# Batched 64x64 matrix products: transposing the second to fourth a tile on VectorE, instead of the third to sixth

## The chip, the cores and the metric

The kernel runs on one core of one Trainium2 chip. The metric is the device time in microseconds (us) of one execution; lower is better. TensorE, VectorE, ScalarE, GpSimd and SyncE are the core's engines; the profile calls them PE (PEld for its weight loads), DVE, ACT, POOL and SP.

## The reference

```python
a = randn(1024, 64, 64)   # float32
b = randn(1024, 64, 64)   # float32
out = np.matmul(a, b)     # 1024 products of 64x64 by 64x64, float32
```

Each input and the output hold 16.78 MB. The products are taken of bf16 casts, with float32 sums.

## The kernel before

**Tiling.** b and the output are cut into 16 steps t of 64 matrices, 1.05 MB each (`n_t = 16`). a is cut into 8 tiles s of 128 matrices (`n_s = 8`), 2.1 MB each, and tile s serves the steps 2s and 2s + 1. The text writes a(s), b(t) and store(t) for these. "The second to fourth a tile" are s = 1, 2, 3; "the third to sixth" are s = 2 to 5.

**Loads.** `load_a(s)` (L70) makes four DMAs: three quarters of the tile go from GpSimd's queue (q0 in the profile), cast to bf16 on the way, into a_sb (L74), and the fourth from SyncE's queue (q1) as float32 into a_raw (L78). Both pools have three buffers (`A_AHEAD = 3`). `load_first_a` (L81) loads tile 0 as float32 into two output buffers. `load_b(t)` (L94) loads one float32 tile b_sb, for even t from SyncE's queue, for odd t from ScalarE's (q10), into one of three buffers (`B_AHEAD = 3`). Every DMA stands in the program of the engine that issues it, so it goes only after that engine has passed the instructions ahead of it, and when its buffer is free.

**From a to the weights.** Each product needs a transposed. There are two ways to it:

- Over TensorE: `regroup(s)` (L100) puts the four quarters side by side into a_bf, with two VectorE copies (L109 from a_sb, L112 from a_raw with a cast; tile 0 has casts of its own, L106). Then `transpose(s, j)`, j = 0 and 1 (L133), makes 8 TensorE transposes (L138) of pairs of bf16 numbers taken as one float32, and two ScalarE copies (L141) from PSUM (at_ps) to at_sb.
- On VectorE: `transpose_dve(s, half)` (L116) transposes two of the four quarters with one VectorE instruction each (L128, 32x32 blocks). The fourth quarter (h = 3), loaded as float32, is first cast to bf16 by ScalarE (L126).

`ON_DVE` lists the tiles that take the second way. From at_sb, `spread(t)` (L146) copies with VectorE into at_bd, one of two block-diagonal buffers whose zeros are set once: 4 copies of 32 x 1024 (L164) for a tile that came over TensorE, 8 copies of 32 x 512 (L154) for one from VectorE.

**Cast, product, output.** `cast(t)` (L169) casts b_sb to b_bf on VectorE (step 0 on ScalarE, the last step in four pieces on both). `multiply(t)` (L187) makes 64 TensorE products in two halves into two PSUM buffers (o_ps), and copies each half to an output buffer o_sb with four copies (L206). These run on ScalarE; of the second half, two go to VectorE in odd steps past the VectorE tiles:

```python
if half and t % 2 and t > 2 * max(ON_DVE):
    copies[2:] = [nc.vector.tensor_copy] * 2
```

so in steps 11 and 13 before. Step 15, the last, has copies of its own on both engines, in quarters. `store(t)` (L183) writes o_sb from GpSimd's queue one step later (`HOLD = 2`); the last two outputs go in smaller pieces, from SyncE's and ScalarE's queues.

**Order.** `manual_schedule()` keeps the order of the program on each engine; nothing is reordered. In step t come, in this order: spread(t + 1), cast(t + 1), load_b(t + 3), in even steps load_a(t/2 + 4) (while there are tiles left) and the second half of tile t/2 + 1's TensorE transposes, multiply(t), then work on tile s + 2 (in even steps regroup or the first VectorE half, in odd steps the first TensorE transposes or the second VectorE half), and store(t - 1). Step 0 prepares tile 1 after its product, and step 1 all of tile 2 if VectorE takes it. GpSimd's queue thus holds load_a(4), store(0), load_a(5), store(1), store(2), load_a(6) and so on; SyncE's a_raw and the even b tiles in turn.

Of the kernel before, what the change touches and what calls it, by code (L numbers as in the profile page):

```python
# [13 lines left out]
def kernel(  # L14
# [21 lines left out]
    B_AHEAD = 3  # L36
    N_BD = 2
    HOLD = 2
    ON_DVE = (2, 3, 4, 5)

    a_v = a.rearrange("(s g h) (mp v) k -> s h g mp (v k)", h=4, g=32, v=16)
    b_v = b.rearrange("(t g h) (kp u) n -> t (h kp) g (u n)", h=4, g=16, u=2)
# [19 lines left out]
    a_tiles, b_tiles, abf_tiles, at_tiles, bbf_tiles = {}, {}, {}, {}, {}  # L62
# [7 lines left out]
    def load_a(s):  # L70

        a_sb = a_pool.tile([128, 3, 16, 64], bf16, name="a_sb")
        for h in range(3):
            nc.gpsimd.dma_start(  # L74
                out=a_sb[:, h, :, :].rearrange("p v k -> p (v k)"), in_=a_v[s, h], single_packet=True
            )
        a_raw = a_pool.tile([128, 16, 64], fp32, name="a_raw")
        nc.sync.dma_start(out=a_raw[:].rearrange("p v k -> p (v k)"), in_=a_v[s, 3])  # L78
        a_tiles[s] = a_sb, a_raw

    def load_first_a():  # L81

        raw = [
            o_pool.tile([128, 8, 2, 2, 64], fp32, name="o_sb")[:].rearrange(
                "p gh j wl n -> p (gh j wl n)"
            )
            for _ in range(2)
        ]
        parts = [raw[h % 2][:, 1024 * (h // 2) : 1024 * (h // 2) + 1024] for h in range(4)]
        for h in range(4):  # L90
            (nc.scalar if h % 2 else nc.sync).dma_start(out=parts[h], in_=a_v[0, h])
        a_tiles[0] = parts

    def load_b(t):  # L94
        b_sb = b_pool.tile([128, 16, 128], fp32, name="b_sb")
        queue = nc.scalar if t % 2 else nc.sync
        queue.dma_start(out=b_sb[:], in_=b_v[t])  # L97
        b_tiles[t] = b_sb

    def regroup(s):  # L100
        a_sb = a_tiles.pop(s)
        a_bf = work.tile([128, 16, 4, 64], bf16, name="a_bf")
        if s == 0:
            for h in range(4):
                copy = nc.scalar.copy if h % 2 else nc.vector.tensor_copy
                copy(a_bf[:, :, h, :], a_sb[h].rearrange("p (v k) -> p v k", v=16))  # L106
        else:
            cast_sb, raw = a_sb
            nc.vector.tensor_copy(  # L109
                a_bf[:, :, 0:3, :], cast_sb[:].rearrange("p h v k -> p v h k")  # L110
            )
            nc.vector.tensor_copy(a_bf[:, :, 3, :], raw[:])  # L112
        abf_tiles[s] = a_bf
        at_tiles[s] = work.tile([128, 32, 4, 4, 4], fp32, name="at_sb")

    def transpose_dve(s, half):  # L116
        cast_sb, raw = a_tiles[s]
        if half == 0:
            at_tiles[s] = work.tile([128, 4, 8, 4, 4, 4], fp32, name="at_sb")
        for h in (2 * half, 2 * half + 1):  # L120
            rows = cast_sb[:, h, :, :] if h < 3 else None
            if h == 3:
                rows = work.tile([128, 16, 4, 64], bf16, name="a_bf")[:, 0:4, :, :].rearrange(
                    "p x y k -> p (x y) k"
                )
                nc.scalar.copy(rows, raw[:])  # L126
            pairs = rows.rearrange("p v k -> p (v k)").bitcast(fp32)
            nc.vector.transpose(  # L128
                at_tiles[s][:, h].rearrange("p g w mp vo -> p w vo g mp"),
                pairs.rearrange("p (vo w kp) -> p w vo kp", vo=4, w=4),  # L130
            )

    def transpose(s, j):  # L133
        a_cols = abf_tiles[s][:].rearrange("p v h k -> p v (h k)").bitcast(fp32)
        for wl in range(2):
            at_ps = t_psum.tile([128, 4, 128], fp32, name="at_ps")
            for vo in range(4):
                nc.tensor.transpose(  # L138
                    at_ps[:, vo, :], a_cols[:, 4 * vo + 2 * j + wl, :], identity[:]
                )  # L140
            nc.scalar.copy(  # L141
                at_tiles[s][:, :, 2 * j + wl, :, :],
                at_ps[:].rearrange("p vo (g mp) -> p g mp vo", mp=4),
            )

    def spread(t):  # L146
        bd = bd_tiles[t % N_BD]
        at_sb = at_tiles[t // 2]
        for h in range(4):
            rows = slice(32 * h, 32 * h + 32)  # L150
            if t // 2 in ON_DVE:
                for i in range(2):
                    block = 32 * (2 * (t % 2) + i)
                    nc.vector.tensor_copy(  # L154
                        bd[rows, 8 * i : 8 * i + 8, :, h, :, :].rearrange(
                            "p g w mp vo -> p (g w) (mp vo)"
                        ),
                        at_sb[block : block + 32, h].rearrange(
                            "p g w mp vo -> p (g w) (mp vo)"
                        ),  # L160
                    )
            else:
                half = slice(16 * (t % 2), 16 * (t % 2) + 16)
                nc.vector.tensor_copy(  # L164
                    bd[rows, :, :, h, :, :].rearrange("p g w mp vo -> p (g w) (mp vo)"),
                    at_sb[rows, half].rearrange("p g w mp vo -> p (g w) (mp vo)"),
                )

    def cast(t):  # L169
        b_bf = work.tile([128, 16, 128], bf16, name="b_bf")  # L170
        b_sb = b_tiles.pop(t)
        if t < n_t - 1:
            (nc.vector.tensor_copy if t else nc.scalar.copy)(b_bf[:], b_sb[:])  # L173
        else:
            for gq in range(4):
                rows = slice(4 * gq, 4 * gq + 4)
                if gq % 2:
                    nc.vector.tensor_copy(b_bf[:, rows, :], b_sb[:, rows, :])
                else:
                    nc.scalar.copy(b_bf[:, rows, :], b_sb[:, rows, :])  # L180
        bbf_tiles[t] = b_bf

    def store(t):  # L183
        for piece in held.pop(t):
            piece()

    def multiply(t):  # L187
# [20 lines left out]
        for half in range(2):  # L208
# [19 lines left out]
            if not last:  # L228
                copies = [nc.scalar.copy] * 4
                if half and t % 2 and t > 2 * max(ON_DVE):  # L230
                    copies[2:] = [nc.vector.tensor_copy] * 2
# [7 lines left out]
    with tc.manual_schedule():  # L239
        load_first_a()  # L240

        nc.vector.memset(warm[:, 0:1], 0.0)
        nc.scalar.copy(warm[:, 1:2], warm[:, 0:1])
        load_b(0)
        load_b(1)
        nc.vector.memset(bd_tiles[0][:], 0.0)  # L246
        make_identity(nc, identity)
        nc.gpsimd.memset(bd_tiles[1][:, 0:8], 0.0)
        load_a(1)
        load_b(2)  # L250
        nc.gpsimd.memset(bd_tiles[1][:, 8:16], 0.0)
        load_a(2)
        regroup(0)
        transpose(0, 0)
        transpose(0, 1)
        spread(0)
        cast(0)
        for t in range(n_t):
            s, half = t // 2, t % 2
            if t + 1 < n_t:  # L260
                spread(t + 1)
                cast(t + 1)
            if t + B_AHEAD < n_t:
                load_b(t + B_AHEAD)
            if half == 0 and 0 < s < n_s - 1 - A_AHEAD:
                load_a(s + 1 + A_AHEAD)
            if half == 0 and 0 < s < n_s - 1 and s + 1 not in ON_DVE:
                transpose(s + 1, 1)
            multiply(t)
            if t == 0:  # L270
                regroup(1)
                load_a(A_AHEAD)
                load_a(A_AHEAD + 1)
                transpose(1, 0)
                transpose(1, 1)
            if t and s + 2 in ON_DVE and (half or s):
                for part in [0, 1] if t == 1 else [half]:
                    transpose_dve(s + 2, part)
                if half:
                    a_tiles.pop(s + 2)  # L280
            elif half == 0 and 0 < s and s + 2 < n_s:
                regroup(s + 2)
            elif half == 1 and s + 2 < n_s:
                transpose(s + 2, 0)
            if t >= HOLD - 1:
                store(t - HOLD + 1)
        for t in range(n_t - HOLD + 1, n_t):
            store(t)
# [30 lines left out]
```

## Time and profile before

| | before |
|---|---|
| time, median of 3 runs | 134.39 us (134.0 to 134.44) |
| profiled execution: its time / its span | 134.24 / 132.1 us |
| VectorE busy | 100.7 us (76%) |
| ScalarE busy | 89.2 us (68%) |
| TensorE busy, weight loads | 63.2 us (48%), 60.5 us (46%) |
| GpSimd busy | 32.0 us (24%) |
| DMA: q0 (GpSimd), q1 (SyncE), q10 (ScalarE) | 50.6%, 30.8%, 20.0% of 16 engines' span |
| read from and written to memory | 33.55 MB and 16.78 MB |
| TensorE clock granted, mean | 0.693 |

The profile's page gives busy times, the span in 40 slices (3.3 us each; digits are tenths of busy time), the DMA queues, the chain of waits that ended last, and groups of instructions ("out<-in", partitions x elements, count, busy time, mean ns of one, idle time of the engine before them and what ended it). L numbers are lines of the kernel. Each b tile takes 14.4 to 26.3 us from its issue to its landing; the first multiplication starts at 21.09 us.

### The profile page before, as it was taken

The page shows a single profiled execution, that of the slowest core. Times are in us where ns is not written, and L with a number is a line of the kernel's source. Part 1 is how long each engine was busy: PE and PEld are TensorE (multiplying, and loading weights), DVE is VectorE, ACT ScalarE, POOL GpSimd, SP SyncE. Part 2 cuts the span into 40 slices and gives each one's busy share as a digit, 9 for nine tenths or more (in the row PEclk, how much of TensorE's full clock was granted, in tenths as well). Part 3 has the DMA queues.
Part 4 walks back from the last instruction along what each step waited for, and adds up shares of the span by engine and source line. Part 5 has one row for each costly group of instructions (what it writes and reads, how often), then busy time and mean ns, then how long its engine had stood idle before and what let it go on. Part 6 is the DMA issues. An engine that isn't in the chain of part 4 may idle for free.

```text
span 132.1 us, 2719 instructions
## 1 busy us (share of the span) xinstructions
PE 63.2 (48%) x1088; PEld 60.5 (46%) x1088; DVE 100.7 (76%) x150; ACT 89.2 (68%) x159; POOL 32.0 (24%) x43
## 2 busy tenths in 40 slices
PE   0006406990733701909190737359709834677700
PEld 0006306980733701909190737259709734676700
DVE  5930399209999915999989998999999998598730
ACT  2225524999893790583989197929999996728970
POOL 8991000420074000702061302040203040312000
PEclk9999999999686555555555555555995995555555
DMA  3999999999999999999999999999999999999996
GB/s 83 351 336 310 309 313 277 288 301 327 326 305 385 371 308 298 395 385 396 327 282 357 402 395 347 296 326 387 399 392 394 394 392 387 398 399 396 364 324 201
DMA packets 19020, 44.99 MB, mean 341 GB/s; under 512 B 1088, under 2 KB 3136, under 8 KB 19008
## 3 DMA queue, kind: packets, MB, share of 16 engines
q0 software_dynamic: 6832, 20.19, 50.6%
q1 hardware_dynamic: 7120, 14.68, 30.8%
q10 hardware_dynamic: 5056, 9.96, 20.0%
q8 instruction: 8, 0.13, 0.4%
q14 instruction: 4, 0.03, 0.1%
HBM read 33.55 MB, written 16.78 MB: 381 GB/s over the span
## 4 chain that ended last, share of the span: by engine, by line
DMA 37%; DVE 27%; ACT 13%; PE 9%; issue 8%; ACTq 2%; SPq 1%
DMA b_sb<-in_b_dram 31%; DVE at_bd L154 11%; ACT o_sb L206 11%; DMA o_sb<-in_a_dram 6%; DVE b_bf L173 6%; PE o_ps L218 5%; DVE at_bd L164 4%; PE at_ps L138 3%; DVE at_sb L128 3%; DVE a_bf L109 1%; DVE a_bf L112 1%; ACTq L97 1%; ACT a_bf L126 1%; ACT a_bf L106 1%; ACT at_sb L141 1%
## 5 line engine op out<-in xcount | busy, mean ns | idle before, releaser
L206 ACT COPY o_sb<-o_ps 64x512 f32<-64x512 f32 x116 | 67.4, 581 | 19.2 <-PE o_ps L218 16.1
L218 PEld LDWEIGHTS <-at_bd 128*128 128x128 bf16 x1024 | 50.5, 125 | 52.9 <-DVE b_bf L173 44.7
L218 PE MATMUL o_ps<-b_bf,at_bd 128*128 128x64 bf16 x960 | 49.1, 231 | 49.4 <-DVE b_bf L173 42.7
L164 DVE COPY at_bd<-at_sb 32x1024 f32<-32x1024 f32 x32 | 23.2, 724 | 12.7 <-ACT at_sb L141 11.9
L154 DVE COPY at_bd<-at_sb 32x512 f32<-32x512 f32 x64 | 27.9, 436 | 1.3
L195 POOL DMA_DIRECT2D out_dram<-o_sb x14 | 15.5, 1108 | 47.5 <-ACT o_sb L206 30.7
L74 POOL DMA_DIRECT2D a_sb<-in_a_dram x21 | 12.4, 606 | 39.8 <-DVE at_sb L128 26.4
L173 DVE CAST b_bf<-b_sb 128x2048 bf16<-128x2048 f32 x14 | 17.2, 1227 | 6.4 <-DMA b_sb<-in_b_dram 6.0
L138 PE MATMUL at_ps<-identity,a_bf 128*128 128x128 f32 x64 | 11.2, 349 | 11.2 <-ACT a_bf L106 11.2
L138 PEld LDWEIGHTS at_ps<-identity,a_bf 128*128 128x128 f32 x64 | 10.3, 188 | 11.1 <-issue 11.1
L128 DVE STREAM_TRANSPOSE at_sb<-a_sb 128x512 f32<-128x512 f32 x12 | 12.0, 1062 | 0.0
L141 ACT COPY at_sb<-at_ps 128x512 f32<-128x512 f32 x16 | 8.5, 594 | 2.1 <-PE at_ps L138 2.0
L106 ACT CAST a_bf<-o_sb 128x1024 bf16<-128x1024 f32 x2 | 2.1, 1044 | 5.2 <-DMA o_sb<-in_a_dram 5.2
L128 DVE STREAM_TRANSPOSE at_sb<-a_bf 128x512 f32<-128x512 f32 x4 | 4.2, 1053 | 0.7 <-ACT a_bf L126 0.7
L126 ACT CAST a_bf<-a_raw 128x1024 bf16<-128x1024 f32 x4 | 4.2, 1046 | 0.7 <-DMA a_raw<-in_a_dram 0.6
L173 ACT CAST b_bf<-b_sb 128x2048 bf16<-128x2048 f32 x1 | 1.9, 1898 | 3.7 <-DMA b_sb<-in_b_dram 3.7
L206 DVE COPY o_sb<-at_ps 64x256 f32<-64x256 f32 x8 | 3.4, 422 | 1.3 <-PE at_ps L218 1.2
L246 DVE MEMSET at_bd<- 128x4096 f32 x1 | 3.5, 3472 | 0.8 <-issue 0.8
L218 PE MATMUL at_ps<-b_bf,at_bd 128*128 128x64 bf16 x64 | 3.6, 242 | 1.0 <-DVE at_bd L164 1.0
L106 DVE CAST a_bf<-o_sb 128x1024 bf16<-128x1024 f32 x2 | 2.8, 1385 | 1.7 <-DMA o_sb<-in_a_dram 1.7
L206 ACT COPY o_sb<-at_ps 64x256 f32<-64x256 f32 x8 | 2.9, 367 | 0.1
L180 ACT CAST b_bf<-b_sb 128x512 bf16<-128x512 f32 x2 | 1.1, 616 | 2.8 <-DMA b_sb<-in_b_dram 2.8
(16 smaller groups left out, 15.4 us busy)
## 6 DMA issues: line engine op xcount, KB each, us to landing
out_dram<-o_sb POOLq DMA_DIRECT2D x14, 1024.0 KB, 21.1
a_sb<-in_a_dram POOLq DMA_DIRECT2D x21, 256.0 KB, 16.0
a_raw<-in_a_dram SPq DMA_DIRECT2D x7, 512.0 KB, 16.9
o_sb<-in_a_dram SPq DMA_DIRECT2D x2, 512.0 KB, 5.8
o_sb<-in_a_dram ACTq DMA_DIRECT2D x2, 512.0 KB, 7.1
out_dram<-o_sb SPq DMA_DIRECT2D x2, 512.0 KB, 3.6
out_dram<-o_sb SPq DMA_DIRECT2D x2, 256.0 KB, 3.6
out_dram<-o_sb ACTq DMA_DIRECT2D x2, 256.0 KB, 3.1
```

Of the source, the lines that this page charges most:

```text
L74: nc.gpsimd.dma_start(out=a_sb[:, h, :, :].rearrange("p v k -> p (v k)"), in_=a_v[s, h], single_packet=True)
L106: copy(a_bf[:, :, h, :], a_sb[h].rearrange("p (v k) -> p v k", v=16))
L126: nc.scalar.copy(rows, raw[:])
L128: nc.vector.transpose(at_tiles[s][:, h].rearrange("p g w mp vo -> p w vo g mp"), pairs.rearrange("p (vo w kp) -> p w vo kp", vo=4, w=4),)
L138: nc.tensor.transpose(at_ps[:, vo, :], a_cols[:, 4 * vo + 2 * j + wl, :], identity[:])
L141: nc.scalar.copy(at_tiles[s][:, :, 2 * j + wl, :, :], at_ps[:].rearrange("p vo (g mp) -> p g mp vo", mp=4),)
L154: nc.vector.tensor_copy(bd[rows, 8 * i : 8 * i + 8, :, h, :, :].rearrange("p g w mp vo -> p (g w) (mp vo)"), at_sb[block : block + 32, h]. ...
L164: nc.vector.tensor_copy(bd[rows, :, :, h, :, :].rearrange("p g w mp vo -> p (g w) (mp vo)"), at_sb[rows, half].rearrange("p g w mp vo -> p ...
L173: (nc.vector.tensor_copy if t else nc.scalar.copy)(b_bf[:], b_sb[:])
L195: store_queue(t, lo).dma_start(out=o_v[t, :, lo : lo + n, :], in_=o_sb[:, lo : lo + n].rearrange("p gh j wl n -> p (gh j wl n)"),)
L206: copies[2 * par + wl](dst, src)
L218: nc.tensor.matmul(o_ps[:, gl, g % 2, j, :], at_bd[:, j, g, :, u], b_bf[:, g, 64 * u : 64 * u + 64], start=(u == 0), stop=(u == 1),)
```

## The change

`ON_DVE` becomes (1, 2, 3). Tile 1, which went over TensorE after product 0, is transposed on VectorE there; tiles 4 and 5 go over TensorE, by the loop's own conditions. Three things follow without an edit of their own: steps 2 and 3 spread with 8 copies instead of 4, and steps 8 to 11 with 4 instead of 8; the test on max(ON_DVE) is now true in steps 7, 9, 11 and 13; and tile 1's a buffers become free for load_a(4) when the transposes (and ScalarE's cast of the fourth quarter) have read them.

```diff
-    ON_DVE = (2, 3, 4, 5)
+    ON_DVE = (1, 2, 3)
...
             multiply(t)
             if t == 0:
-                regroup(1)
+                transpose_dve(1, 0)
+                transpose_dve(1, 1)
+                a_tiles.pop(1)
                 load_a(A_AHEAD)
                 load_a(A_AHEAD + 1)
-                transpose(1, 0)
-                transpose(1, 1)
```

## The prediction

> **What bounds it now.** I read the page's slices first, then its HBM line and the chain that ended last.
>
> ```profile
> DMA  3999999999999999999999999999999999999996
> GB/s 83 351 336 310 309 313 277 288 301 327 326 305 385 371 308 298 395 385 396 327 282 357 402 395 347 296 326 387 399 392 394 394 392 387 398 399 396 364 324 201
> HBM read 33.55 MB, written 16.78 MB: 381 GB/s over the span
> DMA 37%; DVE 27%; ACT 13%; PE 9%; issue 8%; ACTq 2%; SPq 1%
> ```
>
> The DMA engines are full from the second slice to the second last. The dips in GB/s mislead: a_sb lands as bf16, so its packets count half of what they read. Counted by bytes read (an a_sb packet of 2048 as 4096), the trace's packets give 385 to 418 KB in nearly every us from 8 to 123. The bytes are 50.33 MB before and after the change; at 397 KB/us they alone are 126.8 us of the 132.1 us span. The rest is the start, and this end:
>
> ```profile
> core 0: us, PE busy (x) PEld busy (x) DVE busy (x) ACT busy (x) POOL busy (x), PEclk, DMA share, GB/s
> 119.00:124.00 5.00, 4.05 (x77) 3.89 (x75) 3.69 (x8) 4.62 (x8) 0.87 (x1) 0.50 1.01 390
> 124.00:132.00 8.00, 0.74 (x14) 0.57 (x11) 2.47 (x6) 4.10 (x11) 0.00 (x0) 0.50 0.83 284
> ```
>
> Beside the full DMA engines runs a second chain. In the chain view in order of time, VectorE works nearly without a stop from the landing of b(4) until it frees the buffer of b(15):
>
> ```profile
> 24.87 26.29 DMA b_sb<-in_b_dram
> 51.18 1.23 DVE b_bf L173
> ...
> 97.80 1.24 DVE b_bf L173
> ...
> 104.84 14.37 DMA b_sb<-in_b_dram
> 119.25 0.04 issue
> ```
>
> So a lighter VectorE between 51 and 105 brings the last load forward; whether that shortens the kernel is for the full DMA engines to say.
>
> **The change in engine time.** The rows, with shapes apart:
>
> ```profile
> L154 DVE COPY at_bd<-at_sb 32x512 f32<-32x512 f32 x64 | 27.9, 436 | 1.3
> L164 DVE COPY at_bd<-at_sb 32x1024 f32<-32x1024 f32 x32 | 23.2, 724 | 12.7 <-ACT at_sb L141 11.9
> L141 ACT COPY at_sb<-at_ps 128x512 f32<-128x512 f32 x16 | 8.5, 594 | 2.1 <-PE at_ps L138 2.0
> L126 ACT CAST a_bf<-a_raw 128x1024 bf16<-128x1024 f32 x4 | 4.2, 1046 | 0.7 <-DMA a_raw<-in_a_dram 0.6
> L206 DVE COPY o_sb<-o_ps 64x512 f32<-64x512 f32 x4 | 2.8, 690 | 0.1
> L109 DVE COPY a_bf<-a_sb 128x3072 bf16<-128x3072 bf16 x3 | 2.9, 955 | 0.0
> L112 DVE CAST a_bf<-a_raw 128x1024 bf16<-128x1024 f32 x3 | 2.4, 809 | 0.0
> ```
>
> A tile on VectorE costs it 4 transposes (16.2 us for 16: 4.05) and 16 copies of 0.436 (6.98): 11.0 us. A tile over TensorE costs VectorE two regrouping copies (0.955 + 0.809) and 8 of 0.724 (5.79): 7.55 us. One tile fewer saves 3.5. Since max(ON_DVE) falls from 5 to 3, steps 7 and 9 also hand two output copies each to VectorE: 4 x 0.690 = 2.8 more. Net -0.7 us on VectorE. ScalarE: +4 x 0.594 - 1.046 = +1.33 for the tile, -4 x 0.581 = -2.32 for the output copies: -1.0.
>
> By place it is more. Between 51 and 105 VectorE loses the transposes of tiles 4 and 5 (8.1) and 0.6 in each spread of steps 8 to 11 (2.4), and gains two regroupings (3.5) and the 2.8: -4.2 us of the 53.6. ScalarE has +2.7 - 2.3 there. TensorE's 16 transposes of a tile took 1.95 to 3.65 us in the four tiles of the trace; it is 48% busy, so I put them at nothing on the path, at worst 1.8 us for the 8 ahead of a product.
>
> The rows for the transposes alone: 4.05 us on VectorE against 1.95 to 3.65 on TensorE and 2.4 on ScalarE. The Trainium skill (VectorE: DVE Perf Modes, The three transpose paths) speaks against giving a tile to TensorE: 390 ns there, 311 on VectorE for 128 x 128. By it 16 of them a tile would add an estimated 1.3 us of engine time for the one tile more, without the copies out of PSUM.
>
> **Tile 1, early.** Cast(1) ends at 22.4. The three transposes from a_sb fit into 22.4 to 25.4, where VectorE now regroups and then idles 6.0 us for ScalarE's at_sb copies. The fourth needs ScalarE's cast, queued behind the eight output copies of product 0, which end at 27.74: cast to 28.8, transpose to 29.9, spread(2) with eight copies to 33.4, cast(2) from there instead of 32.71. Tile 2 and spread(3) then follow, and cast(3) comes at 42.3 instead of 40.54. The next wait hides this: b(4) lands at 51.16 and VectorE idles 4.24 us ahead of it, of which some 2 remain. Without that cover it would cost the 2 us.
>
> Loads of tile 4: GpSimd's wait for the transposes until 25.4 instead of 23.25, with store(0) behind them, due at 28.03 anyway. SyncE's a_raw(4) waits for ScalarE until 28.8 instead of 23.86, and b(4) stands behind it. Both cost nothing: SyncE's DMA queue is then working through b(2), a_raw(2) and a_raw(3), and a_raw(3) lands at 38.17; GpSimd's has a_sb(3) until 32.97.
>
> **Tiles 4 and 5, late.** Three measured rules of the b loads (1.05 MB each): from issue to first packet 4.0 to 4.2 us (80.16 to 84.3, 94.00 to 98.2, 104.84 to 109.0); 100 KB/us while all three queues have work, 137 while the other b queue is empty; landing 1.5 to 2.5 us after the last packet. Run over the issue times of the trace they put b(15)'s last packet at 117.8; the trace has it at 117.7. The two b queues are now empty in turns (80.5 to 84.3, 86.4 to 91.4, 92.4 to 98.2, 100.1 to 103.2, 107.4 to 109.0), since the next cast comes too late, and stores take the room.
>
> With the change, step 5 has no transposes on VectorE, so spread(7) starts at 66.0 instead of 68.46; cast(7) at 69.5 (b(7) landed at 69.13). Then each cast starts at the later of its landing and VectorE's own work (spread 2.9 to 3.1, cast 1.23, regrouping 1.8 or output copies 1.4):
>
> | load | issue, was | issue | last packet, was | last packet | lands, was | lands |
> |---|---|---|---|---|---|---|
> | b(11) | 80.2 | 76.9 | 92.4 | 90.9 | 94.9 | 93.4 |
> | b(12) | 87.5 | 84.3 | 100.1 | 97.5 | 101.9 | 99.4 |
> | b(13) | 94.0 | 90.4 | 107.4 | 104.0 | 109.6 | 106.2 |
> | b(14) | 99.1 | 96.0 | 113.0 | 109.7 | 115.2 | 111.8 |
> | b(15) | 104.8 | 102.0 | 117.7 | 114.7 | 119.2 | 116.2 |
>
> Load_a(7) comes some 6 us earlier (tile 4 is free after its regrouping at 61.3 instead of 67.3), behind b(8) on SyncE and ahead of store(5) on GpSimd as before; both queues hold work then, so nothing moves.
>
> **The end.** The code after b(15) is the same, so the compute chain to the span's end (12.9 us from landing) would end 3.0 us earlier. The bytes don't allow it. At 119.2 the trace has 4.1 MB to move: 2.0 in q0's packets of 4096 (397 KB/us: 5.0 us) and the 2.1 MB of the last two outputs in packets of 1024 (about 340 KB/us: 6.2 us). That is 11.2 us; it took 11.7, to the last packet at 130.9. The difference is mostly the us from 125 to 126, with 262 KB, when q0 had run dry and the next piece was not yet copied out. An earlier b(15) leaves more stores in q0 and closes this hole: -0.5 us, and no more. Against it: some 9 us change from two busy queues to three, and beside stores the packets gave 390.6 KB/us with three (29 slices) against 398.7 with two (18): +0.2. Sum: -0.3 us. The profiled execution took 134.24 us, 2.1 around its span and 0.15 under the median of 134.39: I predict 133.9.
>
> The trace's stores take 169 ns for 4096 bytes, 24.2 GB/s an engine. The Trainium skill (DMA: Bandwidth & Descriptors, Specifications) gives a ceiling of 435 GB/s for 16 engines; at that rate the last 4.1 MB would take an estimated 9.4 us instead of 11.2 and the sum would be near -2 us. No us of the trace holds such a rate for long, so the measured rate decides.
>
> **Rivals.**
> - Nothing moves: the hole at 125 stays in another place, since output pieces still come one by one, or the three-queue loss eats it. 134.2. For it: each term is under half a us, the runs before spread over 0.44.
> - The compute tail decides, the whole 3.0 us: 131.2. For it: the chain view runs through b(15). Against: no us between 8 and 123 shows free DMA engines.
> - ScalarE holds back the loads, slower. b(11), b(13) and b(15) are issued by ScalarE, behind output copies and now also behind two at_sb copies in steps 7 and 9, which wait for TensorE. If its queue doesn't run ahead to the issue, b(11) goes at 78.1 and b(13) at 91.0, still early. From a further slip of 2 to 3 us on it decides: then they go after 80.2 and 94.0, and 2 us of lateness at two loads moves b(15) by about 1: 135.2. Against: step 11 has this form already, and there b(15) went at 104.84, 0.08 us after cast(12) had freed its buffer, while the two at_sb copies ahead of it still ran.
>
> **Chances.** Forecast 0.50, nothing moves 0.28, compute tail 0.06, ScalarE (and what else delays loads) 0.16. A measurement of this kernel tells about 0.3% (0.4 us) from no change. The forecast is 0.4% under the median; of its 0.50 I give 0.10 to within the bound. Faster 0.40 + 0.06 = 0.46; same 0.28 + 0.10 = 0.38; slower 0.16. The forecast's own range is 133.4 to 134.2 (gain 0.1 to 0.6, and the runs' spread). Stretched to half of the slower case and a little to the other side: 133.2 to 135.0, which leaves out about 0.14.
>
> **What would show it.** Right: VectorE's wait before cast(4) near 2 us, b(4) landing within 0.3 of 51.2; cast(7) at 69.5; b(15) landing near 116; DMA slices full with no hole near 125; span near 131.8. Wrong: a b queue empty for longer than now after 76, b(15) landing at 119 or later, or a span 1 us or more from 132.1 with DMA still full, which would mean that the rate of the packets is no constant.

## The result and the profile after

| | before | after |
|---|---|---|
| time, median of 12 runs each | 134.34 us (133.97 to 135.1) | 133.65 us (133.49 to 133.98) |
| ratio to before, 95% interval | 1 | 0.9954 (0.9943 to 0.9965) |
| profiled execution: time / span | 134.24 / 132.14 us | 133.61 / 131.82 us |

The kernel became 0.5% faster. Of the 0.63 us between the two profiled executions 0.32 lie in the span (first to last instruction) and 0.31 around it. The page's slices, HBM line and chain after:

```profile
DMA  3999999999999999999999999999999999999993
GB/s 68 372 334 313 306 313 280 280 311 321 327 299 400 362 306 297 393 393 400 321 285 357 403 395 362 308 299 385 395 391 393 390 390 397 399 395 406 390 383 136
HBM read 33.55 MB, written 16.78 MB: 382 GB/s over the span
DMA 53%; ACT 15%; DVE 14%; PE 6%; issue 5%; SPq 2%; ACTq 0%; DVEq 0%
```

VectorE's share of the chain fell from 27% to 14%, DMA's rose from 37% to 53%: VectorE now waits for b(9) at 83.6 us, where it worked nearly without a stop before. The chain in order of time (start, us, what; ... marks lines left out):

```profile
29.93 21.27 DMA b_sb<-in_b_dram
51.20 0.02 issue
51.23 1.23 DVE b_bf L173
...
66.47 17.10 DMA b_sb<-in_b_dram
...
102.47 14.73 DMA b_sb<-in_b_dram
117.20 0.02 issue
```

b(4) is issued 5 us later than before (29.93 against 24.87) and lands at the same time; b(15) is issued 2.4 us earlier (102.47 against 104.84) and lands 2.0 us earlier (117.20 against 119.21). VectorE's waits for loads stand in the timeline; the first line is cast(4) before, the others are cast(4) and cast(9) after:

```profile
51.18 1.23 DVE L173 CAST b_bf<-b_sb 128x2048 bf16<-128x2048 f32 x1 [4.24 <-DMA b_sb<-in_b_dram]
```

```profile
51.23 1.23 DVE L173 CAST b_bf<-b_sb 128x2048 bf16<-128x2048 f32 x1 [2.04 <-DMA b_sb<-in_b_dram]
83.66 1.23 DVE L173 CAST b_bf<-b_sb 128x2048 bf16<-128x2048 f32 x1 [1.63 <-DMA b_sb<-in_b_dram]
```

The groups with shapes apart show what VectorE pays:

```profile
L164 DVE COPY at_bd<-at_sb 32x1024 f32<-32x1024 f32 x40 | 29.6, 739 | 6.6 <-ACT at_sb L141 5.6
L154 DVE COPY at_bd<-at_sb 32x512 f32<-32x512 f32 x48 | 22.0, 457 | 1.1
L206 DVE COPY o_sb<-o_ps 64x512 f32<-64x512 f32 x8 | 5.5, 690 | 0.2
L109 DVE COPY a_bf<-a_sb 128x3072 bf16<-128x3072 bf16 x4 | 4.2, 1045 | 0.0
L112 DVE CAST a_bf<-a_raw 128x1024 bf16<-128x1024 f32 x4 | 3.1, 775 | 0.0
```

The counts are those of the change. Several means rose (L164 from 724 to 739, L154 from 436 to 457, L109 from 955 to 1045 ns). The stretches at the end, with the DMA share and GB/s last:

```profile
core 0: us, PE busy (x) PEld busy (x) DVE busy (x) ACT busy (x) POOL busy (x), PEclk, DMA share, GB/s
119.00:124.00 5.00, 1.38 (x48) 1.26 (x44) 3.45 (x9) 4.86 (x11) 0.00 (x0) 1.00 1.02 402
124.00:132.00 8.00, 0.00 (x0) 0.00 (x0) 0.00 (x0) 2.17 (x6) 0.00 (x0) 0.50 0.77 273
```

### The profile page after: what moved, and what is told of

Its sections match the earlier page's. It is cut to its first block, busy times and chain, and to the rows that moved or that the text cites. A ratio compares the mean times of both kernels' runs of the same rounds, so it can differ in the third digit from the quotient of the medians.

```text
span 131.8 us, 2750 instructions
## 1 busy us (share of the span) xinstructions
PE 59.6 (45%) x1104; PEld 56.7 (43%) x1104; DVE 101.8 (77%) x144; ACT 88.1 (67%) x158; POOL 31.9 (24%) x43
## 4 chain that ended last, share of the span: by engine, by line
DMA 53%; ACT 15%; DVE 14%; PE 6%; issue 5%; SPq 2%; ACTq 0%; DVEq 0%
DMA b_sb<-in_b_dram 53%; ACT o_sb L206 12%; PE o_ps L218 6%; DVE at_bd L164 4%; DVE b_bf L173 4%; DVE at_bd L154 2%; ACT b_bf L173 1%; DVE at_sb L128 1%; DVE o_sb L206 1%; DVE a_bf L109 1%; SPq L91 1%; ACT a_bf L126 1%; SPq L97 1%; ACT b_bf L180 1%; DVE a_bf L112 0%
## 5 line engine op out<-in xcount | busy, mean ns | idle before, releaser
L206 ACT COPY o_sb<-o_ps 64x512 f32<-64x512 f32 x112 | 65.0, 581 | 17.9 <-PE o_ps L218 13.5
L218 PEld LDWEIGHTS <-at_bd 128*128 128x128 bf16 x1024 | 45.2, 117 | 52.6 <-DVE b_bf L173 40.5
L218 PE MATMUL o_ps<-b_bf,at_bd 128*128 128x64 bf16 x960 | 45.6, 223 | 48.7 <-DVE b_bf L173 35.0
L164 DVE COPY at_bd<-at_sb 32x1024 f32<-32x1024 f32 x40 | 29.6, 739 | 6.6 <-ACT at_sb L141 5.6
L154 DVE COPY at_bd<-at_sb 32x512 f32<-32x512 f32 x48 | 22.0, 457 | 1.1
L138 PE MATMUL at_ps<-identity,a_bf 128*128 128x128 f32 x80 | 12.9, 329 | 11.0 <-ACT a_bf L106 11.0
L141 ACT COPY at_sb<-at_ps 128x512 f32<-128x512 f32 x20 | 10.8, 591 | 2.7 <-PE at_ps L138 2.0
L128 DVE STREAM_TRANSPOSE at_sb<-a_sb 128x512 f32<-128x512 f32 x9 | 8.9, 1065 | 0.0
L206 DVE COPY o_sb<-o_ps 64x512 f32<-64x512 f32 x8 | 5.5, 690 | 0.2
L106 ACT CAST a_bf<-o_sb 128x1024 bf16<-128x1024 f32 x2 | 2.1, 1045 | 5.0 <-DMA o_sb<-in_a_dram 5.0
L109 DVE COPY a_bf<-a_sb 128x3072 bf16<-128x3072 bf16 x4 | 4.2, 1045 | 0.0
```

The costliest lines, as they stand in the source:

```text
L109: nc.vector.tensor_copy(a_bf[:, :, 0:3, :], cast_sb[:].rearrange("p h v k -> p v h k"))
L128: nc.vector.transpose(at_tiles[s][:, h].rearrange("p g w mp vo -> p w vo g mp"), pairs.rearrange("p (vo w kp) -> p w vo kp", vo=4, w=4),)
L138: nc.tensor.transpose(at_ps[:, vo, :], a_cols[:, 4 * vo + 2 * j + wl, :], identity[:])
L141: nc.scalar.copy(at_tiles[s][:, :, 2 * j + wl, :, :], at_ps[:].rearrange("p vo (g mp) -> p g mp vo", mp=4),)
L154: nc.vector.tensor_copy(bd[rows, 8 * i : 8 * i + 8, :, h, :, :].rearrange("p g w mp vo -> p (g w) (mp vo)"), at_sb[block : block + 32, h]. ...
L164: nc.vector.tensor_copy(bd[rows, :, :, h, :, :].rearrange("p g w mp vo -> p (g w) (mp vo)"), at_sb[rows, half].rearrange("p g w mp vo -> p ...
```

## Experiments

Ratios are to the kernel before on the same chip, with 95% intervals. A diff starts from the kernel before, unless the text or its comment names the changed kernel. The theory: the lighter VectorE from 51 us on brings b(15) forward; then the bytes limit what that is worth.

**Parts of the change.** The late part alone:

```diff
-    ON_DVE = (2, 3, 4, 5)
+    ON_DVE = (2, 3)
```

> Only the late part of the change: ON_DVE = (2, 3), tile 1 over TensorE as before. Theory (the lighter VectorE from 51 us on brings b(15) forward, and the bytes then limit the gain): tiles 4 and 5 do it all, so the ratio is that of the whole change, 0.995 to 0.996, with VectorE's wait before cast(4) near 4.2 us again and b(15) landing within 0.5 us of 117.2. Rival (the gain comes from tile 1, whose transposes fill VectorE's early idle time): 1.000.

Measured: 1.0058 (1.0038 to 1.0079). b(15) landed at 116.7, earlier than in the changed kernel, as the theory has it, yet the kernel became slower than before. Neither theory nor rival had this.

The early part alone:

```diff
-    ON_DVE = (1, 2, 3)        # the changed kernel
+    ON_DVE = (1, 2, 3, 4, 5)
```

> Only the early part: ON_DVE = (1, 2, 3, 4, 5) with tile 1 transposed on VectorE in step 0; the test on max(ON_DVE) then stays as before. Theory: the wait before cast(4) shrinks from 4.2 to about 2 us and nothing else moves; ratio 0.999 to 1.001, b(15) landing near 119.2. Rival (tile 1 brings the gain): 0.995 to 0.996.

Measured: 1.001 (0.9995 to 1.0025), the wait before cast(4) 2.03 us, b(15) landing at 119.4. Tile 1 alone brings nothing. The even ratio hides two shifts: the twelve spans average 132.5 us, 0.5 longer than those of the kernel before, run beside it, and the time around the span is 0.3 shorter. "Nothing else moves" thus held for the time, not for the span.

The changed kernel with the output copies of steps 7 and 9 back on ScalarE:

```diff
-                if half and t % 2 and t > 2 * max(ON_DVE):
+                if half and t % 2 and t > 10:
```

> The changed kernel with the output copies of steps 7 and 9 all on ScalarE again (the test reads t > 10). VectorE has 2.8 us less between 51 and 105, ScalarE 2.3 more. Theory: b(15) lands between 116.2 and 118.2, and the time is that of the changed kernel, 0.995 to 0.997. Rival (the copies handed to VectorE are what pays, since ScalarE held something up): back at 0.999 to 1.001.

Measured: 0.9975 (0.9955 to 0.9995), b(15) landing at 116.4. The interval overlaps both the theory's range (0.995 to 0.997) and the lower end of the rival's (0.999 to 1.001). The profiled execution, with 133.37 us, was among the fastest of twelve that went up to 134.5, and the twelve spans average 131.97 us against 131.98 before. So b(15) doesn't need these copies, but whether the gain within the span does is open.

**Where e1's time went.** Its trace has one more instruction fetch. In the list of DMA queues the first line is of the changed kernel, the second of e1 (packets, MB, share of 16 engines):

```profile
q8 instruction: 8, 0.13, 0.4%
```

```profile
q8 instruction: 9, 0.15, 0.4%
```

These packets hold 16 KB, and each kept a DMA engine for 0.9 to 1.1 us in every trace here. Between two of them lie 129 to 291 TensorE and weight-load instructions of the traces, in two cases of three 258 to 291. A sixth tile over TensorE makes its program long enough for a ninth fetch, at 123.6 us. Each DMA has 16 landings in the trace, read here as one from each DMA engine, and they show what that does. At e1's last but one piece to land (131.44) they spread from -1.4 to +1.2 us around their median, and the last piece to land ended at 131.74, with one engine 2.2 us behind the median. In the changed kernel the last piece ended at 130.91, with the last engine 0.7 behind. Two kernels put this to the test. One has tile 1 over TensorE as before and five TensorE tiles, so exactly the changed kernel's TensorE count:

```diff
-    ON_DVE = (2, 3, 4, 5)
+    ON_DVE = (2, 3, 4)
```

> ON_DVE = (2, 3, 4) in the code of before: tile 1 over TensorE, one tile fewer on VectorE late, and TensorE's program exactly as long as in the changed kernel (five tiles over TensorE). Theory (e1 lost to a ninth instruction fetch of 16 KB at 123.6 us, which TensorE's longer program causes and which holds one DMA engine for 1.1 us when nothing is left to even it out): no fetch on q8 after 116, ratio 0.995 to 0.998 as the changed kernel. Rival (tile 1 on VectorE is what keeps the gain, e1 lost it with that): 1.003 to 1.007 as e1.

The other is the changed kernel with a longer TensorE program that does nothing:

```diff
                 transpose_dve(1, 1)
                 a_tiles.pop(1)
+                for v4 in range(4):
+                    spare = t_psum.tile([128, 4, 128], fp32, name="at_ps")
+                    cols = abf_tiles[0][:].rearrange("p v h k -> p v (h k)").bitcast(fp32)
+                    for vo in range(4):
+                        nc.tensor.transpose(spare[:, vo, :], cols[:, 4 * v4 + vo, :], identity[:])
```

> The changed kernel with 16 idle TensorE transposes (no one reads them) after product 0, where TensorE waits anyway; its program becomes as long as e1's. Theory (late fetch): a ninth fetch on q8 near 122 to 124, one DMA engine 1 us behind the others at the last output, 0.6 to 1.3 us slower than the changed kernel of this call. Rival (tile 1 matters, program length doesn't): same time as the changed kernel within 0.2 us.

With them ran the changed kernel itself:

> The changed kernel once more, as a base on the chip of this call. Ratio 0.994 to 0.998, DMA engines' landings of the last output spread over 1 to 2 us.

Measured: the changed kernel 0.9935 (0.991 to 0.9959), a little under its expected range, ON_DVE = (2, 3, 4) 0.9941 (0.9917 to 0.9964) with its last fetch at 114.3, the longer program 1.0055 (1.0035 to 1.0076), 1.5 us slower than the changed kernel by the medians (135.03 against 133.51). Its ninth fetch came at 123.2, took 1.08 us, and one engine was 1.8 us behind the median at 131.58. So tile 1 is no condition of the gain, and 16 idle transposes early in the program cost more than the change brings. The late fetch shows as 0.9 us in the last landing (131.75 against 130.88), of 1.12 us between the two profiled executions; the rest of these lies behind the last landing (1.17 us to the span's end against 0.92), in SyncE's final waits, which it takes one by one (about 0.06 us each), so that a piece waited for first and landing late puts the others behind it: e1's span ends 1.35 us after its last landing, that of e4 (below) 1.34, the changed kernel's 0.9. A late fetch alone need not cost: the kernel before has its eighth at 120.0 and still lands its last piece within 0.2 us on all 16, after the hole at 125.

**Bytes or tail.** An earlier b(15) by other means, with VectorE's work as before:

```diff
-    B_AHEAD = 3
+    B_AHEAD = 4
...
-    o_pool = ctx.enter_context(tc.tile_pool(name="o_pool", bufs=8))
+    o_pool = ctx.enter_context(tc.tile_pool(name="o_pool", bufs=7))
...
         load_a(2)
+        load_b(3)
```

> The kernel before with a fourth b buffer (B_AHEAD = 4, one output buffer fewer, b(3) loaded ahead of the loop). The b queues no longer run empty in turns, without any change of VectorE's work: b(15) lands some 4 us or more before 119.2. Theory (bytes limit): whatever it lands at, the gain is that of the hole at 125 us and of the ragged end, 0.6 to 1.2 us: ratio 0.991 to 0.996. Rival (the compute tail of 12.9 us after b(15) sets the time): the whole 4 us or more, 0.97 or less.

Measured: 1.0053 (1.0032 to 1.0073). b(15) landed at 111.8, 7.4 us earlier than before, and the last piece at 131.15 against 131.21, though it was issued at 123.2 against 128.3 and so took some 8 us from issue to landing. So past some point an earlier b(15) is worth nothing. It missed the expected gain as well: the packets moved 345 to 381 KB in each us from 119 to 128, where the changed kernel's moved 376 to 414. Why is open.

Then fewer bytes, in both kernels: output 8 is not written, so these two return an incomplete result.

```diff
         for piece in held.pop(t):
-            piece()
+            if t != 8:
+                piece()
```

> The kernel before with output 8 not written (1.05 MB less to move, 2.6 us at 397 KB/us). b(15) still lands near 119.2, since the stores only leave their share of q0 later. Theory (in the kernel before the two bounds meet: the bytes end when the compute tail does): the tail of 12.9 us from b(15) now sets the end, so little is gained: ratio 0.996 to 1.000. Rival (bytes alone set the end of the kernel before too): 0.980 to 0.983.

> The changed kernel with output 8 not written. Theory: here the bytes alone set the end, and the compute tail has room: b(15) lands near 117.2, the last piece is issued near 126.3 and lands about 2.9 us later as it did before under light load, so the span loses some 1.7 of the 2.6 us: ratio to before 0.980 to 0.985. Rival (the changed kernel is held by its compute tail, and closing the hole was all there was): 0.992 to 0.996.

Measured: before without the 1.05 MB 1.0003 (0.9986 to 1.002), no gain at all; the changed kernel without it 0.9819 (0.9786 to 0.9851), 2.5 us under before. The whole change had taken 0.7 of these, so the bytes are worth some 1.8 us of the 2.6 that they take (1.7 was expected). The stretches of the first show why:

```profile
core 0: us, PE busy (x) PEld busy (x) DVE busy (x) ACT busy (x) POOL busy (x), PEclk, DMA share, GB/s
119.00:124.00 5.00, 3.83 (x73) 3.67 (x71) 3.71 (x7) 4.89 (x9) 1.36 (x1) 0.50 0.61 211
124.00:132.00 8.00, 0.82 (x16) 0.66 (x13) 2.53 (x6) 3.52 (x10) 0.00 (x0) 0.50 0.82 276
```

With fewer stores the DMA engines fall idle (share 0.61 from 119 to 124, nothing moved at 120) and the end stays: b(15) landed at 118.6 and the last output follows by the chain of casts, products and copies. The same edit in the changed kernel moves the last landing from 130.91 to 128.50, 2.4 us, of which 0.4 is lost behind it (the span ends 1.35 us after it, not 0.91). The same stretches there:

```profile
119.00:124.00 5.00, 0.76 (x27) 0.64 (x22) 3.24 (x8) 4.86 (x10) 0.00 (x0) 0.90 0.92 337
124.00:132.00 8.00, 0.00 (x0) 0.00 (x0) 0.00 (x0) 1.46 (x4) 0.00 (x0) 0.51 0.52 174
```

How long the last piece takes from issue to landing says the same: 2.94 us before and 2.96 here, 4.64 in the changed kernel, where it queues behind other stores.

**Two tries at more**, both from the changed kernel. Output 14 in large packets:

```diff
-        if t < n_t - 2:
+        if t < n_t - 1:
             return nc.gpsimd
...
-            whole = t < n_t - 2
+            whole = t < n_t - 1
```

> The changed kernel with output 14 written whole from GpSimd's queue like those before it, in packets of 4096 instead of 1024. If the packets' rate (397 against 340 to 380 KB/us) decides, the last 1 MB saves 0.1 to 0.4 us: ratio to before 0.992 to 0.996. If the later issue (after all of output 14 is copied, about 123.5) opens a hole where q0 runs dry near 125, it is 0 to 1 us slower than the changed kernel.

Measured: 0.9944 (0.9924 to 0.9964), no different from the changed kernel beside it (0.9935): the us from 124 to 125 moved 330 KB only, and the landing of the last piece was 130.90 as ever.

GpSimd's first loads ahead of its other work:

```diff
+        load_a(1)
         make_identity(nc, identity)
         nc.gpsimd.memset(bd_tiles[1][:, 0:8], 0.0)
-        load_a(1)
```

> The changed kernel with load_a(1) ahead of GpSimd's identity and its half of the zeros: q0 starts to move near 4 us instead of 7. If DMA engines' time sets the end, the idle shares of the first 5 us (164, 246 and 352 KB in the third to fifth us, of 400) come forward: 0.2 to 0.6 us less than the changed kernel, ratio to before 0.990 to 0.993. If tile 0 and b(0) land later for it, cast(4) has 2 us of room; beyond that, no gain, 0.994 to 0.998.

Measured: 0.9943 (0.9923 to 0.9962), a miss. b(0) landed 1.3 us later (20.50 against 19.21), within the 2 us of room, and b(15) at 117.19. q0 moved from 5 us on, but the third to fifth us gained only some 100 KB in all, 0.25 us of DMA time, and the last piece landed at 130.83 against 130.91. No kernel that writes the whole output beat the changed kernel beyond the intervals; (2, 3, 4) is its equal.

## Why the prediction was right, and where not

**The mechanism held.** VectorE's wait before cast(4) was to shrink from 4.24 to some 2 us and was 2.04; b(4) was to land within 0.3 of 51.2 and landed at 51.20, though SyncE issued it 5 us later. cast(7) started at 70.38 (forecast 69.5). The table's issue times were 0.4 to 0.7 us early and its landings 1.0 off or less: b(11) landed at 93.2 (forecast 93.4), b(12) at 100.4 (99.4), b(13) at 106.6 (106.2), b(14) at 112.4 (111.8), b(15) at 117.2 (116.2). The rules from the trace before carry: first packets some 4 us after the issue, 100 and 137 KB/us.

**VectorE's sum was off.** Forecast -0.7 us net, busy time went up, from 100.7 to 101.8 us: the same instructions got longer (40 x 15 ns at L164 and 48 x 21 ns at L154 are 1.6 us). Why is open. By place it still brought b(15)'s issue forward by 2.4 us, for a forecast of 2.8.

**What bounds the kernel before was misread.** The prediction took full DMA slices for bytes that set the end. The kernel before without 1.05 MB took the same time: its end was the compute tail after b(15) (the casts, products and copies up to the last piece), with the bytes just behind. So the rival of the compute tail named the mechanism that gave way, and the bytes named how far: the tail moved by 2.0 us, the span by 0.32. That cap, the prediction's main step, is what e4 (7.4 us earlier, nothing gained) and e10 (fewer bytes, a last landing 2.4 us earlier) show.

**The end's terms.** The hole at 125 is closed: that us moved 378 KB instead of 262. The packets of 1024 moved 369 to 387 KB/us from 125 to 129 instead of the assumed 340 (335 to 358 before, from 126 to 130). That more pieces were queued doesn't explain this alone: e4's were queued too, and moved 345 to 348 from 125 to 129. The loss from three busy queues was smaller than its 0.2 us: from 51 to 119 us of the changed kernel's trace, beside stores, three queues moved 394.5 KB/us and two 397.8 or 397.9 (a queue counts as busy in a us when it moved over 40 KB), which makes less than 0.1 over 9 us. Left out altogether was that the 16 DMA engines don't end together. Before, the last piece's landings lay within 0.2 us of each other, since the hole let the late engines catch up; after, from -1.1 to +0.7 around the median. The median engine's last landing came 0.9 us earlier (131.1 to 130.2), the slowest one's 0.3, and the slowest ends the span. Too low a gain and a missed loss cancelled, so it is in part luck that the span's -0.3 us came true.

**Around the span.** The prediction carried 2.1 us over; it was 1.79. It is 2.10 to 2.12 in the kernel before, e4 and e9, and 1.79 to 1.88 in all others here. The unprofiled runs agree: their averages are 2.11 to 2.12 us for these three kernels and 1.78 to 1.84 for the others. Half of the profiled gain is this, and no run tells what decides it. The sum also has an uneven step: -0.3 us makes 133.9 of the profiled execution's 134.24, but 134.1 of the median of 134.39 that the forecast is for. The median fell by 0.7 us; 0.3 of that is the time around the span, which the sum had as unchanged.

**Rivals.** Nothing moves: excluded by the interval. ScalarE holds back the loads: b(11), b(13) and b(15) were issued at 77.56, 90.82 and 102.47, each within 0.1 us of the end of the cast that frees its buffer. One that the prediction doesn't name is the granted TensorE clock, 0.50 before and 1.00 after from 119 to 124 us: it sets nothing there, since from b(15)'s landing to the issue of the last piece both kernels take 9.1 us. The 1.3 us of engine time that the prediction sets against a tile over TensorE didn't show either: the 80 transposes of five tiles took 12.9 us after, 2.6 a tile, against 4.0 for a tile's four on VectorE.

## What to carry to other kernels

Full DMA engines don't prove that bytes set the end: leave one transfer out and see whether the end moves, or whether the engines just fall idle. Where two bounds lie close, lifting one is worth only the distance to the other, so price the second before counting the first. A DMA queue in order with work ahead hides an issue that comes 5 us late, and program length is a cost of its own when a fetch falls near the end and the DMA engines stay full after it. An even time can hide two shifts, as e2 shows, so compare spans too.

## What the hardware showed that I had not expected

An instruction fetch shares the DMA engines with the data: 16 KB took 0.9 to 1.1 us of one engine, and after the late ones (e1, e7) one landing of 16 came up to 2.5 and 1.8 us behind the median of its piece. The 16 landings of one DMA lay within 0.5 us of each other at 11 us (before), 3.9 us at 113.6, still 1.8 at 125.6, and within 0.2 at the end, after the hole. They came this close again only where the engines had run short of work (before, e9, e10); after, 1.8 us remained. This reads as if each engine keeps a backlog of its own; that is inferred, since the record names no engine for a packet. Shown is that the slowest of 16 landings ends the kernel.
